# The relu of the index products is written back into its PSUM bank

## The chip, the cores and the metric

The kernel runs on one core of a Trainium2 chip. The core has five engines that work at the same time and meet through semaphores: TensorE (matmuls, whose results go to banks of PSUM), VectorE (DVE in the profile), ScalarE (ACT), GpSimd (POOL) and SyncE (SP, which only issues transfers). SBUF and PSUM are its memories on the chip. The metric is the device time of one execution in microseconds (us), and less is better.

## The reference, cut to what matters

The program is one layer of a decoder trunk over 2048 tokens of width 1024: a projection, three mixers side by side (a gated recurrence, a sparse attention, a convolution), an output projection and an MLP. The change lies in the sparse attention's index. For each query it scores all earlier keys and keeps the 256 best of them:

```python
s = jnp.einsum('bqhd,bsd->bqhs', qib.astype(f32), k_idx_f) * (IDX_DIM ** -0.5)
score = jnp.einsum('bqh,bqhs->bqs', wb, jax.nn.relu(s))
score = jnp.where(admissible[None], score, NEG_BIG)
_, sel = lax.top_k(score, topk)
```

There are 8 index heads of width 32. The score is a sum over the heads of a weight per query and head times the relu of the product of query and key.

## The kernel before, in words

The tokens go through in four blocks of 512 (`b`), and the attention in 16 blocks of 128 queries (`j`). The main stream is matmuls: the input projection of all four blocks first (`in_block`, `mm_T` at L350), then for each block the output projection (`out_block`), the first MLP product (`mm_T` at L350) and the second (`n_part` at L1158). Float32 operands are split into a high and a low part, so each product is three matmuls; ScalarE makes the high part and GpSimd, for the most part, the low one (`split`, L256 and L257).

Beside the main stream run generators, one queue for each kind: `idx` (`index_gen`), `tk` (`topk_gen`) and `at` (`attn_gen`). After each unit of the main stream `step()` gives each queue some credit, and each `yield` says what the piece cost; this sets the order in which the program is written down. A scheduler that runs before the kernel then orders each engine's instructions: among those whose operands and buffers it counts as free it prefers the ones written down earlier. On the chip each engine runs its list in that fixed order and waits for semaphores.

`index_gen` is one block of 128 queries. For each chunk of up to 512 keys (`ki`, one buffer) it goes over the 8 heads: a matmul into a PSUM bank (L745), a relu with a scale on ScalarE (L747), and on VectorE a multiplication by the head's weight, which starts (L750) or adds to (L752) the sum `s`. When all chunks are done GpSimd masks the last 128 keys (L756), and `topk_gen` may start: eight passes over `s` that search a threshold (L850 and small operations), then a flag (L862, L864) that decides between an exact and a short ending. Then `attn_gen` computes scores (L898, L900), exponentials (L914), transposes (L920 to L930) and the product with the values (L932) for each of four heads, and writes the result (L952) to the tensor that `out_block` reads. Two buffers hold `s`.

[...] During the input projection the index takes its bank from the tag `at` (two buffers, shared with the attention). Afterwards the tag `ax` has two buffers and the index has one bank of its own:

```python
def ps_ix():
    if px["ax"] == 3:
        return ps_at()
    return px["p"].tile([P, 512], F32, tag="ix", bufs=3 - px["ax"], name=nm("ix"))
```

Query blocks 2 to 5 (48 heads) are indexed in the first part, blocks 6 to 15 (256 heads) in the second.

Of the kernel before, what the change touches and what calls it, by code (L numbers as in the profile page):

```python
# [8 lines left out]
F32 = mybir.dt.float32  # L9
# [6 lines left out]
AF = mybir.ActivationFunctionType  # L16
OP = mybir.AluOpType
# [3 lines left out]
P = 128  # L21
D = 1024
L = 2048
TB = 512
# [53 lines left out]
def trunk(ctx, tc, x, c, ada_w, ada_b, norm_mix_w, norm_mlp_w, w_in, hg_lb_logits,  # L78
# [3 lines left out]
    V, A, G, T = nc.vector, nc.scalar, nc.gpsimd, nc.tensor  # L82
# [22 lines left out]
    def dma(o, i):  # L105
        return nc.sync.dma_start(o, i)  # L106

    def raw32(a):
        return a.bitcast(F32)
# [7 lines left out]
# [4 lines that stand above are left out]
# [600 lines left out]
    def chunks(j):  # L721
        n = nkeys(j)
        return [(cb, cb * TB, min(TB, n - cb * TB)) for cb in range((n + TB - 1) // TB)]
# [6 lines left out]
    def index_gen(k, j):  # L730
        b, jj = divmod(j, 4)
        qi = k.t([96, 8, P], F32R, "qi", 1)
        for s, src in enumerate((0, 0, 1)):
            dma(raw32(qi[s * 32:(s + 1) * 32]), iq_d[b][src, :, :, jj * P:(jj + 1) * P].rearrange("h p t -> p h t"))
        while live["s"] >= k.sbufs:
            yield None
        live["s"] += 1
        s = k.t([P, k.nmax], F32, "s", k.sbufs)
        sc[j] = s
        for cb, c0, w in chunks(j):  # L740
            ki = k.t([P, TB], F32R, "ki", 1)
            dma(raw32(ki[:96, :w]), ki_d[cb][:, :w])
            for h in range(8):
                ps = ps_ix()
                T.matmul(ps[:, :w], qi[:, h, :], ki[:96, :w], start=True, stop=True)  # L745
                r = k.t([P, TB], F32, "r", 2)
                A.activation(r[:, :w], ps[:, :w], AF.Relu, scale=32.0 ** -0.5)  # L747
                iw = iw_s[:, j, h:h + 1]
                if h == 0:
                    V.tensor_scalar(s[:, c0:c0 + w], r[:, :w], iw, None, op0=OP.mult)  # L750
                else:
                    V.scalar_tensor_tensor(s[:, c0:c0 + w], r[:, :w], iw, s[:, c0:c0 + w],  # L752
                                           op0=OP.mult, op1=OP.add)
                if h % 2:
                    yield 1.1 * w * 2
        G.affine_select(s[:, j * P:(j + 1) * P], s[:, j * P:(j + 1) * P], pattern=[[-1, P]],  # L756
                        compare_op=OP.is_ge, fill=NEG_BIG, base=0, channel_multiplier=1)

        idone.add(j)
# [350 lines left out]
    def add_topk(k, js):  # L1110
        for j in js:
            queues["idx"].append(index_gen(k, j))
            queues["tk"].append(topk_gen(k, j))
# [611 lines left out]
```

## Time and profile before

| | |
|---|---|
| time, median of 3 runs | 3166.78 us (3162.09 to 3168.3) |
| the profiled execution's own time | 3161.17 us |
| its span, first to last instruction | 3159.5 us |
| mean granted TensorE clock | 0.956 |
| TensorE busy | 2859.4 us, 91% |
| VectorE busy | 2085.6 us, 66% |
| GpSimd busy | 1715.5 us, 54% |
| ScalarE busy | 1537.0 us, 49% |

The profile is of one execution. Its times count from the first instruction of the span. An engine's share of busy time is an average over parts with different limits, so the stretch in which the changed lines run (to about 2392 us) has to be read by itself.

### The profile page before, as it was taken

Reading aid. Unit: us, or ns where it says so; the run is one execution under the profiler, and the core shown is the slowest. Engines: PE = TensorE matmul, PEld = TensorE weight load, DVE = VectorE, ACT = ScalarE, POOL = GpSimd, SP = SyncE. Lnnn points to the kernel's source line nnn. Section 1 sums busy time; section 2 is a strip of 40 time slices with the busy share of each in tenths; the row PEclk is TensorE's granted clock in tenths of the full one; section 3 lists DMA queues with packets and bytes.
Section 4 is the critical chain, followed back from the end, with each engine's and each line's share of the span. In section 5 each row is a group of like instructions: output and inputs, shape, how many; then the busy total and the mean of one; then the engine's idle time right before and its main releaser. Section 6 shows DMA issues by size and latency. Waiting matters only on the chain.

```text
span 3159.5 us, 50407 instructions
## 1 busy us (share of the span) xinstructions
PE 2859.4 (91%) x18352; PEld 2573.1 (81%) x18352; DVE 2085.6 (66%) x3673; ACT 1537.0 (49%) x2879; POOL 1715.5 (54%) x1231
## 2 busy tenths in 40 slices
PE   5979988898999989999999999998898898889987
PEld 4767868777787879888888889898787888889987
DVE  7785486867436444847776757576979631477787
ACT  3435444445313244555556556455544444456653
POOL 6555162225205255555767566576665656756675
PEclk9989999998999999999999999999999999999998
DMA  7856665564655343434546444455799953455533
GB/s 261 267 175 235 221 191 188 192 214 162 196 195 165 119 151 97 136 118 121 157 140 207 138 124 149 122 163 160 241 284 300 299 184 121 143 192 171 175 113 104
DMA packets 479413, 560.08 MB, mean 177 GB/s; under 512 B 32615, under 2 KB 371884, under 8 KB 479148
## 3 DMA queue, kind: packets, MB, share of 16 engines
q1 hardware_dynamic: 478992, 556.65, 55.9%
q8 instruction: 145, 2.38, 0.3%
q14 instruction: 120, 0.98, 0.1%
q10 hardware_dynamic: 156, 0.07, 0.0%
HBM read 458.30 MB, written 98.31 MB: 176 GB/s over the span
## 4 chain that ended last, share of the span: by engine, by line
PE 54%; DVE 22%; DMA 9%; issue 6%; ACT 4%; POOL 3%; SPq 1%; DVEq 0%; POOLq 0%; ACTq 0%
PE mm L350 18%; PE ax L1158 17%; PE mm L1158 5%; DVE cacc L523 2%; DMA adw<-in_ada_w_dram 2%; DVE s L752 2%; DVE cum L850 2%; DMA tsr<-in_mlp_w_dram 2%; PE po L932 1%; PE ix L745 1%; PE at L920 1%; SPq L106 1%; PE ax L632 1%; PE at L898 1%; DMA wr<-ts_d 1%
## 5 line engine op out<-in xcount | busy, mean ns | idle before, releaser
L257 POOL TENSOR_TENSOR wlo<-wraw,whi 128x1024 fp32r<-128x1024 f32 x257 | 635.5, 2473 | 479.6 <-ACT whi L256 343.0
L256 ACT CAST whi<-wraw 128x1024 fp32r<-128x1024 f32 x257 | 270.0, 1050 | 346.7 <-PE ax L1158 127.7
L752 DVE SCALAR_TENSOR_TENSOR s<-r,iw_s,s 128x512 f32<-128x512 f32 (+3 forms) x266 | 301.9, 1135 | 199.8 <-ACT r L747 197.1
L1158 PE MATMUL ax<-whi,hh 128*128 128x256 f32 x1600 | 282.9, 291 | 43.9 <-DVE acc L1302 32.8
L350 PE MATMUL mm<-ah,wk 128*128 128x512 f32 x1104 | 300.9, 405 | 8.1 <-issue 2.5
L1158 PE MATMUL ax<-whi,hl 128*128 128x256 f32 x1600 | 280.2, 289 | 2.2 <-POOL hl L257 2.2
L1158 PEld LDWEIGHTS ax<-whi,hh 128*128 128x128 f32 x1600 | 237.5, 195 | 54.4 <-DVE acc L1302 33.9
L350 PE MATMUL mm<-ah,whi 128*128 128x512 f32 x936 | 263.2, 406 | 16.3 <-DVE slo L463 9.3
L1158 PE MATMUL ax<-wlo,hh 128*128 128x256 f32 x1600 | 275.1, 287 | 0.0
L930 POOL TENSOR_TENSOR pT<-L,pT 128x512 fp32r<-128x512 f32 (+3 forms) x160 | 202.1, 1266 | 115.7 <-ACT pT L929 107.9
L350 PE MATMUL mm<-ah,wlo 128*128 128x512 f32 x936 | 255.4, 397 | 0.0
L350 PE MATMUL mm<-al,whi 128*128 128x512 f32 x936 | 254.9, 396 | 0.0
L350 PEld LDWEIGHTS mm<-ah,wk 128*128 128x128 f32 x1104 | 206.2, 193 | 51.3 <-issue 3.9
L747 ACT ACTIVATE r<-ix 128x512 f32<-128x512 f32 (+3 forms) x256 | 141.3, 552 | 216.3 <-PE ix L745 196.2
L1158 PEld LDWEIGHTS ax<-whi,hl 128*128 128x128 f32 x1600 | 235.0, 194 | 6.5 <-POOL hl L257 3.2
L1158 PEld LDWEIGHTS ax<-wlo,hh 128*128 128x128 f32 x1600 | 230.9, 193 | 2.2
L521 POOL TENSOR_TENSOR cside<-cside,ctap 128x512 f32<-128x512 f32 x112 | 165.3, 1476 | 120.9 <-ACT ctap L520 98.4
L350 PEld LDWEIGHTS mm<-ah,whi 128*128 128x128 f32 x936 | 177.0, 194 | 54.3 <-DVE slo L463 10.1
L350 PEld LDWEIGHTS mm<-ah,wlo 128*128 128x128 f32 x936 | 177.1, 191 | 37.0 <-POOL wlo L257 0.2
L350 PEld LDWEIGHTS mm<-al,whi 128*128 128x128 f32 x936 | 175.8, 190 | 35.8
L1302 DVE TENSOR_TENSOR acc<-acc,ax 128x512 f32<-128x512 f32 x160 | 109.1, 682 | 90.1 <-PE ax L1158 89.7
L850 DVE TENSOR_SCALAR_CACHE_REDUCE cum<-s,ssm 128x384 bf16<-128x384 f32 (+13 forms) x112 | 165.3, 1476 | 3.3 <-POOL s L756 1.4
(552 smaller groups left out, 6938.2 us busy)
## 6 DMA issues: line engine op xcount, KB each, us to landing
wraw<-in_mlp_w_dram SPq DMA_DIRECT2D x192, 512.0 KB
wk<-wk_d SPq DMA_DIRECT2D x174, 512.0 KB
kc<-sk_d SPq DMA_DIRECT2D x112, 256.0 KB
vc<-v_d SPq DMA_DIRECT2D x112, 256.0 KB
tsr<-in_mlp_w_dram SPq DMA_DIRECT2D x96, 256.0 KB
ts_d<-tsr SPq DMA_DIRECT2D x48, 512.0 KB
wr<-in_mlp_w_dram SPq DMA_DIRECT2D x96, 256.0 KB
wr<-ts_d SPq DMA_DIRECT2D x72, 256.0 KB
```

What stands on the lines that cost most here:

```text
L106: return nc.sync.dma_start(o, i)
L256: A.copy(hi, src)
L257: (lo_eng or G).tensor_tensor(lo, src, hi.bitcast(F32), OP.subtract)
L350: T.matmul(ps, ww[:, k, :], aa[k], start=(n == 0 and k0 == 0), stop=(n == len(order) - 1 and k1 == NK))
L521: G.tensor_tensor(side, side, tap, OP.add)
L523: V.scalar_tensor_tensor(acc, hc[:, w:w + TB], cvc[:, m, w:w + 1], acc, op0=OP.mult, op1=OP.add)
L747: A.activation(r[:, :w], ps[:, :w], AF.Relu, scale=32.0 ** -0.5)
L752: V.scalar_tensor_tensor(s[:, c0:c0 + w], r[:, :w], iw, s[:, c0:c0 + w], op0=OP.mult, op1=OP.add)
L850: V.tensor_scalar(dump, s, t, -AIM - i * STEP, op0=OP.is_ge, op1=OP.add, accum_out=d)
L930: G.tensor_tensor(pT[:, :nt, 1], lv, pT[:, :nt, 0].bitcast(F32), OP.subtract)
L1158: T.matmul(ps[:, t * 256:(t + 1) * 256], aa[f][:, tok * P:(tok + 1) * P], ww[:, f, :], start=(first and n == 0 and (last or t == 0)), stop ...
L1302: V.tensor_tensor(dst, dst, src, OP.add)
```

## The change

The relu no longer writes a tile in SBUF. It writes over its input, in the PSUM bank of the matmul, and VectorE's two operations read that bank.

```diff
             for h in range(8):
                 ps = ps_ix()
                 T.matmul(ps[:, :w], qi[:, h, :], ki[:96, :w], start=True, stop=True)
-                r = k.t([P, TB], F32, "r", 2)
-                A.activation(r[:, :w], ps[:, :w], AF.Relu, scale=32.0 ** -0.5)
+                A.activation(ps[:, :w], ps[:, :w], AF.Relu, scale=32.0 ** -0.5)
                 iw = iw_s[:, j, h:h + 1]
                 if h == 0:
-                    V.tensor_scalar(s[:, c0:c0 + w], r[:, :w], iw, None, op0=OP.mult)
+                    V.tensor_scalar(s[:, c0:c0 + w], ps[:, :w], iw, None, op0=OP.mult)
                 else:
-                    V.scalar_tensor_tensor(s[:, c0:c0 + w], r[:, :w], iw, s[:, c0:c0 + w],
+                    V.scalar_tensor_tensor(s[:, c0:c0 + w], ps[:, :w], iw, s[:, c0:c0 + w],
                                            op0=OP.mult, op1=OP.add)
```

## Rows read from the trace of the kernel before

**Rows 1.** The page's head: span, then busy time, share and instructions of each engine.
```profile
span 3159.5 us, 50407 instructions
PE 2859.4 (91%) x18352; PEld 2573.1 (81%) x18352; DVE 2085.6 (66%) x3673; ACT 1537.0 (49%) x2879; POOL 1715.5 (54%) x1231
```
**Rows 2.** Busy time by windows: length, PE, PEld, DVE, ACT, POOL, granted clock, DMA share, GB/s.
```profile
1177.00:2392.00 1215.00, 1144.30 (x7316) 1034.50 (x7315) 842.33 (x1434) 665.53 (x1202) 762.77 (x508) 0.98 0.53 159
2392.00:2661.00 269.00, 247.36 (x1658) 226.66 (x1656) 139.02 (x231) 128.47 (x227) 168.51 (x106) 0.97 0.75 236
```
**Rows 3.** Groups by form: count, busy us, mean ns, idle before, releaser.
```profile
L752 DVE SCALAR_TENSOR_TENSOR s<-r,iw_s,s 128x512 f32<-128x512 f32 x196 | 246.0, 1255 | 125.5 <-ACT r L747 124.1
L750 DVE TENSOR_SCALAR s<-r,iw_s 128x512 f32<-128x512 f32 x28 | 28.0, 1001 | 31.5 <-ACT r L747 31.3
L747 ACT ACTIVATE r<-ix 128x512 f32<-128x512 f32 x200 | 119.2, 596 | 155.8 <-PE ix L745 139.5 <-DVE s L752 7.6 <-DVE ssm L856 4.8
```
**Rows 4.** Single lines of VectorE: duration in ns, minimum/median/maximum.
```profile
L752 DVE SCALAR_TENSOR_TENSOR s<-r,iw_s,s x266: 333/752/2922, 99.6 to 2391.5; 128x512 f32<-128x512 f32 x100, 128x384 f32<-128x384 f32 x14, 128x128 f32<-128x128 f32 x10, 128x256 f32<-128x256 f32 x9
L687 DVE SCALAR_TENSOR_TENSOR r<-ax,cols,gate x16: 718/744/752, 212.2 to 1163.5; 128x512 f32<-128x512 f32 x16
L1302 DVE TENSOR_TENSOR acc<-acc,ax x160: 659/683/689, 1246.4 to 2648.5; 128x512 f32<-128x512 f32 x160
```
**Rows 5.** Timeline at 1178 us, GpSimd and VectorE: start, length, [idle before, releaser].
```profile
1178.23 2.41 POOL L257 TENSOR_TENSOR wlo<-wraw,whi 128x1024 fp32r<-128x1024 f32 x1 [0.78 <-issue]
1178.53 2.39 DVE L750 TENSOR_SCALAR s<-r,iw_s 128x512 f32<-128x512 f32 x1 [11.72 <-ACT r L747]
```
**Rows 6.** Timeline of TensorE: two pairs of neighbouring index matmuls; the second with all between.
```profile
2126.81 0.40 PE L745 MATMUL ix<-ki,qi 96*128 96x512 f32 x1
...
2130.17 0.40 PE L745 MATMUL ix<-ki,qi 96*128 96x512 f32 x1
...
1223.41 0.34 PE L745 MATMUL ix<-ki,qi 96*128 96x384 f32 x1
1223.59 1.77 PE L350 MATMUL mm<-ah,wlo 128*128 128x512 f32 x7
1225.19 1.98 PE L350 MATMUL mm<-ah,whi 128*128 128x512 f32 x8
1227.01 1.98 PE L350 MATMUL mm<-al,whi 128*128 128x512 f32 x8
1228.82 0.39 PE L350 MATMUL mm<-ah,wlo 128*128 128x512 f32 x1
1229.05 0.34 PE L745 MATMUL ix<-ki,qi 96*128 96x384 f32 x1
```
**Rows 7.** Windows of L745 alone, query block 12: length, PE and PEld busy.
```profile
1763.00:1907.00 144.00, 11.42 (x32) 5.99 (x31) 0.99 0.42 125
```
**Rows 8.** Timeline, last query block: index end, search, flag, attention's end, output projection.
```profile
2392.34 0.29 POOL L756 TENSOR_SCALAR_AFFINE_SELECT s<-s 128x128 f32<-128x128 f32 x1 [3.15 <-DVE s L752]
...
2392.67 2.35 DVE L850 TENSOR_SCALAR_CACHE_REDUCE cum<-s,ssm 128x2048 bf16<-128x2048 f32 x1 [0.40 <-POOL s L756]
...
2446.18 2.35 DVE L850 TENSOR_SCALAR_CACHE_REDUCE cum<-s,ssm 128x2048 bf16<-128x2048 f32 x1
...
2517.49 0.14 DVE L864 CAST far<-at 1x1 uint32<-1x1 f32 x1
...
2660.60 0.37 ACT L952 COPY ot<-at 128x256 f32<-128x256 f32 x1 [0.82 <-PE at L950]
...
2665.91 1.45 PE L1158 MATMUL ax<-whi,mh 128*128 128x256 f32 x4 [5.34 <-ACT mh L256]
```
**Rows 9.** Waits of TensorE, 1177 to 2661 us, the largest for VectorE: total, times, longest.
```profile
PE ax L1158 <- DVE acc L1302: 32.8, 10, 11.5
...
PE at L898 <- DVE mx L900: 9.7, 6, 3.8
PE mm L265 <- DVE ah L274: 8.5, 1, 8.5
```

## The prediction

> **What bounds the kernel now.** I read the page's busy line first. TensorE is busy for 91% of a span of 3159.5 us, VectorE for 66%, GpSimd for 54% [rows 1]: TensorE sets the pace, and an engine behind it matters only where TensorE runs out of ready work. Around the span lie 1.7 us (3161.17 us for the profiled execution, which is 5.6 us under the median of the runs, 3166.78 us).
>
> Next the windows. 256 of the 304 index heads run between 1177 and 2392 us, where TensorE is busy 1144.30 of 1215 us and VectorE 842.33; in the 269 us after that TensorE is busy 247.36 [rows 2]. So TensorE idles some 71 + 22 = 93 us while the index, the threshold search and the attention pass beside the MLP.
>
> Then the timeline of TensorE alone. In this part the index has one PSUM bank (tag ix, one buffer), and the bank goes: matmul, relu on ScalarE, next matmul. A matmul of 0.40 us and a relu of 0.596 us make a round trip of about 1.0 us [rows 3, 6], yet two index matmuls stand 3.36 us apart, and 5.64 us apart where the other matmuls are 512 wide [rows 6]. In between stand 7 + 8 + 8 + 1 = 24 matmuls of the MLP in the second case. The order on TensorE is fixed before the run, and I read this distance as follows: the next index matmul takes its place in the order only when its bank is counted as free, and by then many others stand ahead of it. A block of 32 heads therefore takes 144 us, 4.5 us a head [rows 7], though its matmuls are 11.42 us of work. The index is held by its bank, not by an engine.
>
> Last, the chain to the end. The final index block ends at 2392.3 us, and its threshold search begins 0.33 us later: the search was waiting for the index. The last of its eight passes starts at 2446.2 and lasts 2.35 us; the flag that ends the search is copied at 2517.5, 69 us after that pass; the last attention result is copied at 2660.6, and the output projection of the last token block then waits 5.34 us for data made from it [rows 8]. So the chain index, search, attention and the stock of other TensorE work end at the same time, near 2661 us. Lateness of the index beyond the 69 us is lateness of the end, as far as the tail cannot shrink.
>
> **The change part by part.** *Removed: two SBUF inputs.* L752 reads r and s from SBUF and takes 333 to 2922 ns, median 752; the same operation with one PSUM input, L687, takes 718 to 752, and L1302, a tensor_tensor with one PSUM input, 659 to 689 in 160 instances [rows 4]. What blocks it is GpSimd: the L750 that began 0.3 us after a GpSimd subtraction of 2.41 us took 2.39 us and ended with it [rows 5]. With 744 ns in place of 1255, the 196 instances of 128x512 give back 196 x 0.511 = 100 us of VectorE; the 28 L750 of that width, at 744 in place of 1001, give 7 [rows 3, 4]. That work lies beside TensorE. It can return at most what TensorE waited for VectorE in this stretch, 32.8 + 9.7 + 8.5 = 51 us in its three largest groups [rows 9]. VectorE's work there falls by 107 of 842 us, an eighth; a wait shrinks by more than the mean load does, so I take half, 25 us, between 0 and 51.
>
> [...]
>
> *Moved: relu's output goes to PSUM.* The trace has no ScalarE operation from PSUM to PSUM. Nearest is L747 itself, 596 ns [rows 3]; I take that, within 0.1 us either way, which is part of the bounds below. The two r buffers in SBUF go; no DMA and no matmul is added or removed.
>
> *Added: the bank is held until VectorE has read it.* Its round trip now ends with L752, not with the relu. With VectorE free that adds the 0.744 us of the operation and a hop of about 0.03, 0.77 in all. VectorE is busy 69% of this stretch with instructions of 842.33/1434 = 0.59 us in the mean [rows 2], so a relu finds it busy two times in three with half an instruction left: 0.69 x 0.3 = 0.2 us. I take 1.0 us. The upper bound is 1.9 us, if what stands in front is often a search pass of 2.35 us [rows 8] (0.69 x half of it, 0.8, and a second short one of 0.3).
>
> Queued behind the waiting matmul on TensorE is everything later in its fixed order. I expect the order to move with the bank (the matmul is placed later), so TensorE itself waits little; it is the index that slows. The first head of each chunk of eight is hidden behind the load of its keys (ki has one buffer), so 224 of 256 heads pay: 224 x 1.0 = 224 us (172 to 425). The 48 heads of the first part run on two banks shared with attention, spread over hundreds of us; I take nothing there.
>
> *The sum.* The index ends at 2392 + 224 = 2616 instead of 2392. TensorE's other work runs out near 2630, an estimate: 2661 less the 11 us of index matmuls [rows 7] and some 20 of attention that aren't done by then. From there the tail, 269 us now, has the machine to itself; ScalarE, its busiest helper apart from GpSimd's weight work, was busy 128 us in it with everything [rows 2], so I let the rest of the tail run in proportion to 128 for 269. 14 us at the old pace (5%), then 95% of 128 = 121: attention ends at 2751, 90 us late. Less 25: +65. 3161 + 65 = 3226, by the median of runs 3232; I say 3230.
>
> Low end: 0.77 us a head, index at 2564, 66 us at the old pace, 75% of 128 = 96, attention at 2726, +65, less the whole 51: +14, 3175. High end: 1.9 us, index at 2817 by the old pace; of it 187 us lie beyond 2630, 28 heads at 6.6 us each (4.75 now, 1215/256, and 1.9); alone on the machine they need the round trip of 1.0 + 1.9 = 2.9 us each, 81 us; attention at 2630 + 81 + 128 = 2839, +178, with no relief: 3339.
>
> **The rivals.**
> *A, faster: the block on VectorE decides.* If the distance of index matmuls is set by the pace at which the loop emits heads and not by the bank, nothing slows, and TensorE gets back 25 to 51 us: 3161 - 38 = 3123 us in the middle. For it: instances beyond 2 us are in the rows and gone by the change [rows 4, 5]. Against it: the search starts 0.33 us after the index [rows 8], so the index was awaited. It decides as long as the longer hold is under the slack: 69/224 = 0.3 us a head.
> [...]
> *B, no change.* The hold costs, but the 69 us before the flag and the relief cover it: 3161 within 6 us. It needs about 0.4 us a head, under the 0.77 of an idle VectorE; against it stands that VectorE is 69% busy.
> *C, much slower.* The tail does not shrink, because attention is paced by its own order and not by free engines. Then 224 - 69 = 155 us stay, less 25: 3161 + 130 = 3291; with the hold at 1.9 us 3339 and above. For it: nothing in the order changes after the fact.
> *D, TensorE stands at the bank.* If the fixed order did not move, the index matmul would wait in front of all others; for heads whose VectorE operation was blocked past the next matmul this is a direct stall. At 3.36 us spacing against a new round trip of about 2 us it is rare, so this adds to the forecast rather than replacing it: under 20 us.
>
> **How the numbers follow.** My forecast (index slower, tail shrinks in part, 3175 to 3339 by its bounds) gets 0.55, C 0.15, B 0.08, A 0.22. A time within 0.2% (about 6 us) is what a measurement of this kernel can hardly tell from no change. Faster: A, 0.22. Same: B, 0.08. Slower: forecast and C, 0.70. The range reaches down to 3135, which leaves out about half of A (0.12), and up to 3340, the high end of the sum, which leaves out the upper part of C (0.06). The likeliest case alone is 3175 to 3339.
>
> **What the next profile would show.** Right: L752 has a maximum below 0.8 us and a mean near 0.7; pairs of index matmuls at 4.3 us and more where they stood 3.36 apart; the last index block ending near 2616 us (it was 2392); new TensorE idle time in front of the last attention blocks or the last output projection, some 60 to 100 us. Wrong: index matmuls still 3.4 us apart (rival A), or the index late but the flag of the last block still near 2517 us (B), or large waits of the index matmul itself for VectorE (D). The step I trust least is the last: how far the tail shrinks once TensorE has nothing else.

## The result and the profile after

The kernel after takes 3182.57 us, median of 4 runs (3181.68 to 3184.68), against 3167.54 us for 4 runs of the kernel before on the same chip. The medians are 15 us apart; the ratio of the two sets of runs is 1.0056, with a 95% interval of 1.0041 to 1.0071, which makes 18 us. It is slower, as forecast, and inside the range, but by 15 to 18 us where the forecast was 63. In the listing of the kernel after, line numbers from the relu on are one lower: L746 is the relu, L749 and L751 VectorE's two operations, L755 the mask, L849 the search pass, L861 and L863 the flag, L951 the last attention copy, L1157 the output projection.

The page's head after, to be read against [rows 1]:
```profile
span 3180.0 us, 50095 instructions
PE 2860.4 (90%) x18352; PEld 2574.7 (81%) x18352; DVE 1970.1 (62%) x3673; ACT 1542.8 (49%) x2883; POOL 1668.6 (52%) x1231
```
TensorE's work is the same; VectorE has 115.5 us less of it. So the span grew by idle time of TensorE.

The single lines after, minimum/median/maximum as in [rows 4]:
```profile
L751 DVE SCALAR_TENSOR_TENSOR s<-ix,iw_s,s x224: 349/749/753, 1149.3 to 2572.9; 128x512 f32<-128x512 f32 x89, 128x384 f32<-128x384 f32 x10, 128x128 f32<-128x128 f32 x7, 128x256 f32<-128x256 f32 x6
L746 ACT ACTIVATE ix<-ix x256: 256/582/603, 1142.5 to 2572.3; 128x512 f32<-128x512 f32 x100, 128x384 f32<-128x384 f32 x12, 128x128 f32<-128x128 f32 x8, 128x256 f32<-128x256 f32 x8
```
VectorE's sum never takes longer than 0.753 us; before, it took up to 2.922 [rows 4]. Rows 5 show the block on L750; in the kernel before it stands on the sum L752 as well:
```profile
1183.93 2.40 POOL L257 TENSOR_TENSOR wlo<-wraw,whi 128x1024 fp32r<-128x1024 f32 x1 [1.87 <-PE mm L350]
...
1184.17 2.72 DVE L752 SCALAR_TENSOR_TENSOR s<-r,iw_s,s 128x512 f32<-128x512 f32 x1 [3.25 <-ACT r L747]
```
The sum ends 0.56 us after GpSimd's subtraction. Counted over the 196 sums of 512 columns before, the 60 that met no GpSimd instruction took 0.753 us at most, and all 86 that took more than 1 us met one. After, 88 of the 196 sums of that width met a subtraction of L257, and none took more than 0.753 us. So the sum was blocked with both inputs in SBUF and is not with one of them in PSUM. (L750, with a single tensor as its input, in SBUF, was blocked as well [rows 5].)

The relu over its own bank takes 0.582 us in the mean at 512 columns, against 0.596 where it wrote SBUF [rows 3]:
```profile
L746 ACT ACTIVATE ix<-ix 128x512 f32<-128x512 f32 x200 | 116.4, 582 | 201.2 <-PE ix L745 200.5
```

TensorE's timeline after, one stretch with three index matmuls, to be read against [rows 6]:
```profile
1244.89 0.40 PE L745 MATMUL ix<-ki,qi 96*128 96x512 f32 x1
1245.12 1.09 PE L350 MATMUL mm<-ah,whi 128*128 128x512 f32 x4
1246.05 1.98 PE L350 MATMUL mm<-al,whi 128*128 128x512 f32 x8
1247.87 1.98 PE L350 MATMUL mm<-ah,wlo 128*128 128x512 f32 x8
...
1250.69 0.40 PE L745 MATMUL ix<-ki,qi 96*128 96x512 f32 x1
...
1254.88 0.52 PE L1157 MATMUL ax<-wlo,hh 128*128 128x256 f32 x3
1258.92 0.50 PE L745 MATMUL ix<-ki,qi 96*128 96x512 f32 x1 [3.53 <-DVE s L751]
```
The fixed order did move: 26 other matmuls stand between the first two. Between the second and the third the order did not move far enough, and TensorE stands 3.53 us for the bank. From the first index matmul of the second part (1177.46 us before, 1142.06 after) to the last mask (2392.34 and 2575.15, below) the 256 heads take 1215 us before and 1433 after: 218 us more, 0.85 us a head.

The last query block after, as [rows 8]:
```profile
2575.15 0.29 POOL L755 TENSOR_SCALAR_AFFINE_SELECT s<-s 128x128 f32<-128x128 f32 x1
2575.48 2.35 DVE L849 TENSOR_SCALAR_CACHE_REDUCE cum<-s,ssm 128x2048 bf16<-128x2048 f32 x1 [1.85 <-POOL s L755]
...
2578.61 2.35 DVE L849 TENSOR_SCALAR_CACHE_REDUCE cum<-s,ssm 128x2048 bf16<-128x2048 f32 x1
...
2601.89 2.35 DVE L849 TENSOR_SCALAR_CACHE_REDUCE cum<-s,ssm 128x2048 bf16<-128x2048 f32 x1
...
2604.87 0.15 DVE L863 CAST far<-at 1x1 uint32<-1x1 f32 x1 [0.37 <-PE at L861]
...
2677.70 0.37 ACT L951 COPY ot<-at 128x256 f32<-128x256 f32 x1 [0.96 <-PE at L949]
...
2683.06 2.25 PE L1157 MATMUL ax<-whi,mh 128*128 128x256 f32 x6 [5.39 <-ACT mh L256]
```
The index ends 183 us later, but the attention only 17. From mask to flag it is now 30 us where it was 125, and from flag to the last copy 73 where it was 143: the tail has gone from 268 to 103 us.

TensorE's waits after, 1177 to 2700 us, as [rows 9]:
```profile
PE ix L745 <- DVE s L751: 38.6, 15, 6.7
PE at L861 <- DVE ssm L850: 32.3, 3, 27.9
...
PE ix L745 <- DVE s L749: 8.1, 2, 5.8
```
And the window in which the main stream has run dry, first before, then after (columns as [rows 2]):
```profile
2600.00:2700.00 100.00, 89.26 (x639) 84.21 (x638) 13.82 (x32) 41.61 (x71) 65.43 (x49) 0.93 0.38 123
```
```profile
2600.00:2700.00 100.00, 59.06 (x255) 46.34 (x256) 27.30 (x66) 36.65 (x78) 33.65 (x33) 0.62 0.29 88
```
TensorE is idle for 41 of these 100 us after, 11 before. That is where the lost time lies: TensorE has only the last block's search and attention to wait for.

### The profile page after: what moved, and what is told of

It is laid out like the page before. It is cut to its first block, busy times and chain, and to the rows that moved or that the text cites. A ratio compares the mean times of both kernels' runs of the same rounds, so it can differ in the third digit from the quotient of the medians.

```text
span 3180.0 us, 50095 instructions
## 1 busy us (share of the span) xinstructions
PE 2860.4 (90%) x18352; PEld 2574.7 (81%) x18352; DVE 1970.1 (62%) x3673; ACT 1542.8 (49%) x2883; POOL 1668.6 (52%) x1231
## 5 line engine op out<-in xcount | busy, mean ns | idle before, releaser
L257 POOL TENSOR_TENSOR wlo<-wraw,whi 128x1024 fp32r<-128x1024 f32 x257 | 632.0, 2460 | 513.0 <-ACT whi L256 369.2
L751 DVE SCALAR_TENSOR_TENSOR s<-ix,iw_s,s 128x512 f32<-128x512 f32 (+3 forms) x224 | 155.4, 694 | 310.3 <-ACT ix L746 309.3
L929 POOL TENSOR_TENSOR pT<-L,pT 128x512 fp32r<-128x512 f32 (+3 forms) x160 | 187.9, 1176 | 207.1 <-ACT pT L928 196.5
L1157 PE MATMUL ax<-whi,hh 128*128 128x256 f32 x1600 | 277.2, 290 | 16.3 <-DVE acc L1242 9.9
L1157 PE MATMUL ax<-whi,hl 128*128 128x256 f32 x1600 | 282.4, 290 | 0.3 <-POOL hl L257 0.3
L1157 PE MATMUL ax<-wlo,hh 128*128 128x256 f32 x1600 | 276.2, 289 | 0.0
L1157 PEld LDWEIGHTS ax<-whi,hh 128*128 128x128 f32 x1600 | 235.7, 195 | 24.1 <-DVE acc L1242 10.8
L746 ACT ACTIVATE ix<-ix 128x512 f32<-128x512 f32 (+3 forms) x256 | 138.0, 539 | 226.1 <-PE ix L745 225.1
L1157 PEld LDWEIGHTS ax<-whi,hl 128*128 128x128 f32 x1600 | 236.0, 195 | 3.4 <-POOL hl L257 1.0
L1157 PEld LDWEIGHTS ax<-wlo,hh 128*128 128x128 f32 x1600 | 234.9, 196 | 3.2
L849 DVE TENSOR_SCALAR_CACHE_REDUCE cum<-s,ssm 128x384 bf16<-128x384 f32 (+13 forms) x112 | 165.3, 1476 | 11.5 <-POOL s L755 9.3
```

The source lines that it names most:

```text
L257: (lo_eng or G).tensor_tensor(lo, src, hi.bitcast(F32), OP.subtract)
L746: A.activation(ps[:, :w], ps[:, :w], AF.Relu, scale=32.0 ** -0.5)
L751: V.scalar_tensor_tensor(s[:, c0:c0 + w], ps[:, :w], iw, s[:, c0:c0 + w], op0=OP.mult, op1=OP.add)
L849: V.tensor_scalar(dump, s, t, -AIM - i * STEP, op0=OP.is_ge, op1=OP.add, accum_out=d)
L929: G.tensor_tensor(pT[:, :nt, 1], lv, pT[:, :nt, 0].bitcast(F32), OP.subtract)
L1157: T.matmul(ps[:, t * 256:(t + 1) * 256], aa[f][:, tok * P:(tok + 1) * P], ww[:, f, :], start=(first and n == 0 and (last or t == 0)), stop ...
```

## The experiments

Ratios are to the kernel before, run beside each kernel, with 95% intervals. To compare runs of different chips, the text multiplies differences of ratios by 3167 us.

### Each part alone

**The first part alone** (query blocks 2 to 5, 48 heads; `k1` is the object of that part):
```diff
-                r = k.t([P, TB], F32, "r", 2)
+                r = ps if k is k1 else k.t([P, TB], F32, "r", 2)
```


> The change in the first part alone (48 heads on the two shared banks); the second part keeps its tile in SBUF. Theory 1 (two effects: VectorE is no longer blocked, which speeds the main stream everywhere; the held bank slows the index in the second part, which costs at the end): only the gain is left, about 30 us that the main stream of the changed kernel is ahead after the first part, so about 3137 us, and the second part's index still 3.4 us a head where it is densest. Rival 2 (the 30 us are a chance of the new order and not of the blocked VectorE): within 10 us of the kernel before, 3157 to 3177. Rival 3 (the first part loses too, since its banks are shared with attention): slower than 3170.

Measured: 3111.69 us, 0.9837 (0.9816 to 0.9859). It is faster, by 52 us, and so by some 20 more than theory 1 said.

**The second part alone** (256 heads), the same line with `is not`:

> The change in the second part alone (256 heads on the one bank). Theory 1: the loss without the gain of the first part, 3183 + 30 = about 3210 us; index spacing about 5.6 us in the mean as in the changed kernel, TensorE idle some 60 us before the last output projection. Rival 2 (the first part's 30 us are chance): about 3183. Rival 4 (the bank does not matter, the loss of the changed kernel came from elsewhere): at or under 3167.

Measured: 3220.19 us, 1.0164 (1.0144 to 1.0185), slower by 52 us. The end of its index and of its attention:
```profile
2616.82 0.29 POOL L756 TENSOR_SCALAR_AFFINE_SELECT s<-s 128x128 f32<-128x128 f32 x1 [2.60 <-DVE s L752]
...
2719.53 0.37 ACT L952 COPY ot<-at 128x256 f32<-128x256 f32 x1 [0.96 <-PE at L950]
```
The index ends 224.5 us later than before; the tail is 102.7 us. So 224.5 - (268.3 - 102.7) = 59 us stay at the end of the attention of this execution. (It is the longest of the five; by the ratio 52 us stay.)

The two parts pull in opposite directions, and they nearly add up: in the presence of the second part, the first is worth 1.0056 - 1.0164 = -0.0108, or -34 us.

### Hold and relief apart

**The hold without the relief, second part.** The relu still goes to SBUF and VectorE's sum still has two SBUF inputs, but one added column, read from the bank after the sum, keeps the bank until then:
```diff
                     V.scalar_tensor_tensor(s[:, c0:c0 + w], r[:, :w], iw, s[:, c0:c0 + w],
                                            op0=OP.mult, op1=OP.add)
+                if k is not k1:
+                    hd = k.t([P, 1], F32, "hd", 2)
+                    V.scalar_tensor_tensor(hd, ps[:, :1], iw, s[:, c0:c0 + 1], op0=OP.mult, op1=OP.add)
```


> The kernel before, with the bank of the second part held until VectorE has finished the head: after the weighted sum VectorE reads one column of the bank (256 extra instructions of one element, into a tile that nothing reads). VectorE keeps reading its two operands from SBUF, so GpSimd still blocks it. Theory 1: the cost of the hold without the relief: slower than the second-part-only kernel by the relief, 15 to 45 us, so 3225 to 3255 us; index spacing 5.6 us or more. Rival 4 (the bank does not matter): the extra instructions alone, under 10 us, so 3167 to 3177, with the index as dense as before.

Measured: 3307.16 us, 1.0446 (1.042 to 1.0472). The added group of instructions, the end of the index and that of the attention:
```profile
L756 DVE SCALAR_TENSOR_TENSOR hd<-ix,iw_s,s 128x1 f32<-128x1 f32 x256 | 55.1, 215 | 5.5
```
```profile
2709.53 0.29 POOL L759 TENSOR_SCALAR_AFFINE_SELECT s<-s 128x128 f32<-128x128 f32 x1 [11.67 <-DVE s L752]
...
2812.49 0.37 ACT L955 COPY ot<-at 128x256 f32<-128x256 f32 x1 [0.96 <-PE at L953]
```
The time is 52 us over the range of theory 1. The hold behind a blocked instruction and a second small one moves the index's end by 317 us, and the tail is 103.0 us once more. It adds 55 us of VectorE's time of its own, so it bounds the price of a hold without relief from above.

**The hold without the relief, first part**: the same three lines with `if k is k1:`.

> The kernel before, with the banks of the first part (48 heads, two banks shared with attention) held until VectorE has finished the head, by one extra read of one column into a tile that nothing reads; VectorE still reads two operands from SBUF. The question is where the 54 us of the first-part-only kernel come from. Relief theory (VectorE is no longer blocked by GpSimd): no gain here, 3165 to 3200 us. Order theory (the longer hold makes another order on TensorE, and that order is the better one): the gain shows here too, 3110 to 3140 us.

Measured: 3127.35 us, 0.9882 (0.986 to 0.9905): faster by 37 us with no relief at all. Something else than the block by GpSimd was in it; the experiments on the order, below, say what it was in part.

**SBUF layout.** The first part alone frees the two `r` buffers there; this version fills that room again:
```diff
+        if k is k1:
+            for _ in range(2):
+                V.memset(k.t([P, TB], F32, "pad", 2)[:, :1], 0.0)
```


> The first-part-only kernel, with the SBUF of the tile that it saves filled by two tiles of the same size (one column of each is cleared by VectorE at the start of each query block, 8 tiny instructions). Memory theory (the gain comes from 4 KB a partition that come free, which move other tiles): the gain of 54 us goes, 3150 us or more. Relief theory: it stays, 3105 to 3125 us.

Measured: 3109.9 us, 0.9824 (0.9803 to 0.9846), the same as the first part alone. TensorE's order is the same in these two kernels in all 18352 places. The freed room is not the cause.

### The bank and the pace

**Three banks shared** by the index and the MLP's second product in the second part, in place of two and one, on top of the change:
```diff
-        return px["p"].tile([P, 512], F32, tag="ax", bufs=px["ax"], name=nm("ax"))
+        return px["p"].tile([P, 512], F32, tag="ax", bufs=3, name=nm("ax"))
...
-        return px["p"].tile([P, 512], F32, tag="ix", bufs=3 - px["ax"], name=nm("ix"))
+        return ps_ax()
```


> The changed kernel, but in the second part the index takes its bank from the three that it shares with the second MLP product, in place of one of its own beside two. Theory 1: the index is no longer tied to one bank, so its spacing falls below 5 us, the last block's index ends before 2500 us, and the relief stays: 3100 to 3140 us. Rival 4 (the late index is due to the order in which heads are written down, not to its bank): index spacing as in the changed kernel, 3175 to 3195. Rival 5 (the index takes banks from the MLP product and TensorE waits there): faster index, but TensorE idle on the lines of the MLP product, 3190 or more.

Measured: 3128.35 us, 0.9878 (0.9859 to 0.9897), by the ratios 56 us under the kernel after. The index ends at
```profile
2327.57 0.67 POOL L755 TENSOR_SCALAR_AFFINE_SELECT s<-s 128x128 f32<-128x128 f32 x1 [0.56 <-DVE s L751]
```
248 us earlier than after, with the hold still there. In this kernel the held bank is the delay only while it is the only one.

**Three banks with the relu in SBUF**, the same edit on the kernel before:

> The three shared banks of the second part with the kernel before, so with the tile in SBUF: the control for the changed kernel with three shared banks (3128 us). If the change is worth something once the bank is not scarce, this is slower than 3128 us, by the relief of both parts, 20 to 50 us: 3150 to 3180. If it is not, it is at or under 3128.

Measured: 3174.09 us, 1.0029 (1.0017 to 1.0041). So the banks alone bring nothing, and where the bank is not scarce the change is worth 1.0029 - 0.9878 = 0.0151, or 48 us. Of these, 29 us are there when the first part ends (L687 starts for the last time at 1136.2 us, against 1165.4 in this control). The other 19 come later, but the two kernels also have different orders there, and the next section but one shows that an order can be worth as much. So a gain by the relief in the second part is not shown.

**The pace of the index's queue.** The kernel after with twice the credit for index work in the second part, 1900 in place of 950:
```diff
-R2 = [950, 1650, 900]
+R2 = [1900, 1650, 900]
```


> The changed kernel, with twice the credit for index heads in the second part (1900 in place of 950), so that the program writes them down earlier. Bank theory: the heads wait for their bank in any case; index spacing at its densest as in the changed kernel, last index end within 40 us of 2575, 3165 to 3195 us. Order theory (the heads come late because they are written down late): index end before 2480, time at or under 3150 us.

Measured: 3179.49 us, 1.0039 (1.0023 to 1.0056), with the index's end at 2580.66 us against 2575.15. The edit did not reach the chip: TensorE, VectorE and GpSimd have the same order in both traces, TensorE in all 18352 places. So the credit is not what sets the distance of the heads, and 1.0039 beside 1.0056 shows how far two series of nearly one program can lie apart. What holds the heads back, the three banks say and not this run.

### The slack

**Every second head.** First part changed; in the second only heads 1, 3, 5 and 7:
```diff
-                r = k.t([P, TB], F32, "r", 2)
+                r = ps if k is k1 or h % 2 else k.t([P, TB], F32, "r", 2)
```


> The first part as changed; in the second part only the odd heads are read from the bank, the even ones from a tile in SBUF. Slack theory (attention's tail behind the last index needs at least 103 us and has 268 in the kernel before, so the index may come 165 us late for nothing): index late by half of 225, so about 110 us, near 2460; no loss, and a part of the second part's relief, so 3080 to 3112 us. Proportional theory (each us of index lateness costs, as the prediction had it): 3112 plus half of 54 or more, 3135 to 3165 us.

Measured: 3109.95 us, 0.9824 (0.9804 to 0.9844). First its index and attention ends, then those of the first part alone:
```profile
2448.62 0.68 POOL L756 TENSOR_SCALAR_AFFINE_SELECT s<-s 128x128 f32<-128x128 f32 x1 [3.72 <-DVE s L752]
...
2605.84 0.37 ACT L952 COPY ot<-at 128x256 f32<-128x256 f32 x1 [0.96 <-PE at L950]
```
```profile
2347.85 0.68 POOL L756 TENSOR_SCALAR_AFFINE_SELECT s<-s 128x128 f32<-128x128 f32 x1 [1.35 <-DVE s L752]
...
2611.39 0.37 ACT L952 COPY ot<-at 128x256 f32<-128x256 f32 x1 [0.81 <-PE at L950]
```
An index that ends 101 us later costs nothing that the times show, and the attention ends no later. (The order of the second part differs between the two, so some us either way could hide in it.) The run tells against a price for each us, but the prediction did not claim that: its own sum, with the index at 2449, gives an attention about 11 us late, which this run can't tell from none. More is said by the three kernels in which the index ends 183, 224 and 317 us later than before: the tail is 103 us in each, and the attention ends 17, 59 and 152 us later. The tail did not go under that length, and from there on lateness was paid in full.

### The order itself

A small edit anywhere in the first part can change what the scheduler writes down later. The credit of the index's queue in the first part was moved by 5% in both directions, with nothing of the change:
```diff
-R1 = [1126, 1216, 1594]
+R1 = [1070, 1216, 1594]
```


> The kernel before, with 5% less credit for index heads in the first part (1070 in place of 1126): nothing of the change, a slightly other order of writing down. In the list of instructions TensorE's order differs from that of the kernel before in the first part alone. Order theory (the second part's order of the first-part-only and the hold-first kernels, which has none of the change in it, is worth about 25 us): this kernel has the old second-part order, so 3155 to 3180 us. Noise theory (any new order moves the time by 20 us or more either way): outside that.

Measured: 3159.16 us, 0.9985 (0.9973 to 0.9997). And with 1182 in its place:

> The kernel before, with 5% more credit for index heads in the first part (1182 in place of 1126): nothing of the change. In the list of instructions its second part has, on TensorE, the order of the first-part-only and the hold-first kernels and not that of the kernel before. Order theory: faster by about 25 us, 3130 to 3150 us, and index ends in the second part spaced as in those two kernels. Relief theory (the whole gain of the first-part-only kernel needs the unblocked VectorE): 3160 us or more.

Measured: 3138.91 us, 0.9909 (0.9893 to 0.9925): 29 us less, from a number that changes no instruction's work (the profiled execution is the longest of the six, 3143.38 us). Counted in the traces, the number of TensorE instructions between neighbouring index matmuls of the second part (255 places) agrees within two in all 255 places among this kernel, the first part alone, the padded one and the hold in the first part; it agrees in all 255 between the kernel before and the one with the credit down; and in only 113 across the two groups. So there are two orders of the second part among them. What the second one is worth can be read from when each kernel ends its first part (the last start of L687, the recurrence's last instruction), its index and its attention, in us of one execution each:

| kernel | first part | index | attention |
|---|---|---|---|
| before | 1163.5 | 2392.3 | 2660.6 |
| after | 1127.9 | 2575.2 | 2677.7 |
| first part alone | 1135.4 | 2347.9 | 2611.4 |
| second part alone | 1166.5 | 2616.8 | 2719.5 |
| hold in the first part | 1160.9 | 2362.6 | 2619.4 |
| credit down | 1154.6 | 2386.1 | 2654.5 |
| credit up | 1156.2 | 2378.0 | 2641.3 |

Against the kernel before, the credit-up kernel ends its first part 7 us earlier and its attention 19; the hold in the first part 3 and 41; the first part alone 28 and 49. So behind the first part the three with the second order gain another 12, 39 and 21 us. The order is worth something in all three, but not the same, and the 29 us of the credit-up kernel are not all of the second part.

## Why the prediction was right in sign and wrong in size

**Right: the hold, and its price.** The forecast was 224 us on the index's end; the second part alone measured 224.5, and the kernel after 218 from first matmul to end. Three banks remove it. That the first head of each chunk doesn't pay, and the other 224 do, is borne out as well: summed over the starts of L745, the distances in front of the first heads come to 218 us before and 209 with the second part alone, those in front of the others to 988 and 1226, which is 1.06 us a head where the forecast had 1.0. The match to half a us is luck all the same: the forecast let TensorE wait "little", and in the kernel after it stood at the bank for 47 us.

**The step that failed: "The 48 heads of the first part run on two banks shared with attention, spread over hundreds of us; I take nothing there."** It is the term that was put at nothing: it measured -34 us beside the second part, and -52 alone. L687 ends the first part; it starts for the last time at 1163.5 us before [rows 4], and after, then with the second part alone, then with the hold in the first part at:
```profile
L687 DVE SCALAR_TENSOR_TENSOR r<-ax,cols,gate x16: 726/742/752, 211.6 to 1127.9; 128x512 f32<-128x512 f32 x16
```
```profile
L687 DVE SCALAR_TENSOR_TENSOR r<-ax,cols,gate x16: 714/744/752, 211.5 to 1166.5; 128x512 f32<-128x512 f32 x16
```
```profile
L687 DVE SCALAR_TENSOR_TENSOR r<-ax,cols,gate x16: 731/746/751, 207.1 to 1160.9; 128x512 f32<-128x512 f32 x16
```
So the kernel after begins its second part 39 us before the one with the second part alone, and its index and its attention end 42 us before that one's: the gain is made in the first part and carried to the end. Windows of the time before the second part, before and then after (columns as [rows 2]):
```profile
0.00:1140.00 1140.00, 1002.77 (x5862) 865.44 (x5863) 740.88 (x1590) 465.16 (x968) 449.77 (x399) 0.94 0.60 195
```
```profile
0.00:1140.00 1140.00, 1017.04 (x6020) 878.52 (x6021) 757.15 (x1619) 489.03 (x1013) 462.46 (x420) 0.95 0.63 201
```
By 1140 us TensorE has begun 158 matmuls more. The waits that shrank, in the same stretch, before and then after:
```profile
PE ax L654 <- DVE k L598: 19.4, 6, 6.9
PE ax L640 <- DVE k L598: 14.1, 8, 4.9
PE ax L632 <- DVE k L598: 13.4, 7, 4.0
```
```profile
PE ax L632 <- DVE k L598: 13.7, 9, 2.1
...
PE ax L640 <- DVE k L598: 8.7, 8, 1.8
...
PE ax L654 <- DVE k L598: 7.8, 3, 6.1
```
They fell from 46.9 to 30.2 us. With the second part alone they are 46.2 us. In the three kernels that have another order of the first part and no relief (the hold there, the credit up, the credit down) they are 35.8, 38.5 and 47.7. So half of the fall, or more, can come without relief. For the rest the reading is that VectorE's index work, 48 heads of it, was no longer blocked in front of L598; this is argued from the waits, and no run isolates L598. I had looked for the relief's use in the second part only.

How much of the first part is relief? All six kernels with the first part changed have one order of TensorE there, and end it 27 to 36 us before the kernel before. Three other orders without relief (the hold, the credit down and the credit up) end it 3 to 9 us before it. No kernel has the relief in the old order, or that new order without the relief, so the share of each stays open; that no order without relief came near speaks for the relief. By the times, with the second part's order alike, the first part alone is 14 us under the hold without relief (0.9837 against 0.9882) and 23 under the credit-up kernel (0.9909).

**Wrong, and hidden by another error: the tail.** I let 135 us of it remain (14 at the old pace and 95% of 128); it is 103 in the kernel after, in the second part alone and with the hold alone. "In proportion to 128 for 269" took the busiest engine's total for the path. The rows show a path of dependent instructions: eight passes, most of them 3.9 us apart (2578.61 to 2601.89 is 6 steps of 3.88), make the 30 us to the flag. The slack of the index was therefore not the 69 us after the last pass, but 268 - 103 = 165 us, by the two lengths; where exactly the price begins was not run.

**Wrong, in the other direction: the relief in the second part.** I subtracted 25 us for it at the end. But the price of a head was already that of an unblocked sum (0.744 us), so the relief stood in the sum once. And in every kernel here the span ends 496 to 503 us after the start of the last attention copy, so TensorE's waits for VectorE in front of that end count only as far as they delay it. With the second part alone the last L1302 of the MLP's second product starts 39 us sooner than before, where [rows 4] have 2648.5, and the attention still ends 59 us later:
```profile
L1302 DVE TENSOR_TENSOR acc<-acc,ax x160: 654/686/691, 1248.2 to 2609.4; 128x512 f32<-128x512 f32 x160
```
The relief does work through the index: without it, and with one more read, the hold makes the index 317 us late and not 224.5. A term for it beside that, at the end, no run shows.

So the sum, mended: +224 of index, less 165 of slack, is +59 at the attention's end, +52 in time, less 34 from the first part: +18, as 1.0056 says (0.0056 x 3167 = 17.7). The forecast of +65 would have been near for the second part alone, by two errors that cancel: 31 us too much for the tail, and 25 taken off.

**Two readings of rows.** L750 in rows 5 does not end with the GpSimd instruction but 0.28 us after it. And the 107 us of VectorE's work count all 224 instructions of 512 columns; 200 of them stand in the stretch of the second part (the relu's x200 in rows 3), so 96 us do. Neither changes the result.

**PSUM or SBUF as the source.** For the sum the traces show no difference: at 512 columns the 60 sums that met no GpSimd instruction before have a mean of 746 ns with both inputs in SBUF, and L751 has one of 748 from PSUM. For the multiplication it is otherwise: at 512 columns 16 of the 28 L750 took 470 to 500 ns from SBUF, and L749 takes 746 from PSUM. The mean of 1001 before came from the blocked ones, so the change still gains there.
```profile
L751 DVE SCALAR_TENSOR_TENSOR s<-ix,iw_s,s 128x512 f32<-128x512 f32 x175 | 130.8, 748 | 204.1 <-ACT ix L746 203.0
...
L749 DVE TENSOR_SCALAR s<-ix,iw_s 128x512 f32<-128x512 f32 x25 | 18.6, 746 | 21.5 <-ACT ix L746 21.0
```

**The rivals.** *A, faster by the relief*, fell for this kernel: the bank decides. The 3128 us with three banks are near its 3123 in number only: 29 of those 48 us are the first part's, which A did not have. *B, no change*: fell; its slack was too small in my hands (69 for 165), but so was the first part, and 15 to 18 us are outside its 6. *C, a tail that does not shrink*: fell, most clearly of all; the tail shrank to 103. *D, TensorE standing at the bank*: 38.6 + 8.1 = 46.7 us in 17 waits, more than the "under 20 us" I gave it. It need be no separate loss in this kernel, since TensorE then waits for the last block all the same; that is argued, not run.

## What to carry to other kernels

When a buffer's life gets longer, find how many of it there are: the same edit costs 52 us where the index has one bank, and brings 34 beside that, or 52 alone, where it has two. The slack of a delayed chain is its tail's present length less the length of the tail's own dependent steps (here 268 - 103); compute the second from the instructions, not from an engine's busy share. And where a stage early in the kernel is changed as well, price it by itself, by when it ends. And before a gain of one per cent is credited to an edit in a kernel with a scheduled order, change the order by something meaningless: here 5% of a credit was worth 29 us. The best versions here, the change in the first part alone or with every second head as well, take 3110 us, 1.8% under the kernel before. About half of that is there when the first part ends; of what comes after it, the order alone can make the most.

## What was not expected of the hardware

A relu from PSUM over its own bank is not dearer than one into SBUF (0.582 against 0.596 us at 512 columns). In the kernel before, a VectorE sum that began while GpSimd's subtraction ran waited it out: the 74 sums of 512 columns that began in one of L257 ended at least 0.54 us after it, the 28 that took over 2.3 us 0.54 to 0.56 us after one, and the sum alone takes 0.75. A VectorE multiplication by a weight per row takes 0.746 us at 512 columns from PSUM and about 0.485 from SBUF where nothing blocks it. The added VectorE read of a single column took 0.215 us in the mean, 256 of them 55 us; these small reads were not free.

And the granted clock of TensorE was 0.62 in the 100 us after 2600, in which it was busy for 59 and waited for the last block, against 0.93 before, where it was busy for 89. The windows in front of the fall and behind it, in the kernel after (columns as [rows 2]):
```profile
2540.00:2577.00 37.00, 33.59 (x268) 32.42 (x266) 14.42 (x25) 21.29 (x40) 24.36 (x20) 1.00 0.51 155
```
```profile
2578.00:2628.00 50.00, 11.61 (x36) 8.31 (x37) 38.34 (x78) 6.38 (x14) 2.54 (x2) 0.50 0.13 40
```
The granted clock was 1.00 in the 37 us up to 2577, past the end of the last index block (2575.44); then TensorE stood 27.9 us for the search, and in the 50 us from 2578, in which the attention behind it began, the clock was 0.50. So the 103 us of the tail are in part at the lower clock; what they would be at the higher one was not run.
